# Starting six weight buffers at different offsets modulo 256 bytes

## Chip, cores and metric

The kernel runs on one core of a Trainium2 chip. The metric is the device time of one execution in microseconds (us), the median of several runs. PE is TensorE's matmul side, PEld its weight loads, DVE VectorE, ACT ScalarE, POOL GpSimd, SP the engine that issues most DMAs.

## What is computed

Two transformer blocks on one sequence of 256 positions and 2048 channels, all in 32-bit floats. The first has a hybrid mixer (pooling and a gated delta net), cross attention to a memory of 256 positions and a gated feed-forward; the second has adaptive norms from a conditioning vector, a mixer of two sparse attentions, and a feed-forward with a squared relu. Cut to its products with the large weights:

```python
p = h @ w_in                                   # 2048 x 5136, first mixer
x = x + concat([y_pool, y_dn]) @ w_mix_out
x = x + attention(h @ w_xq, mem_h @ w_xkv) @ w_xo
x = x + (silu(dwconv(h @ w_gate)) * (h @ w_up)) @ w_down     # width 5632
p2 = h2 @ w_in_2 ; x = x + gate * norm(mixers(p2) @ w_o_2)
x = x + gate * norm(relu(h2 @ w_up_2) ** 2 @ w_down_2)       # width 8192
```

## The kernel before

**Tiling.** A weight matrix is cut into groups of 512 columns and each group into units of two blocks of 128 rows, so a unit is 128 partitions by 1024 floats (512 KB). 880 units come through the same ten buffers: four buffers `w32` as the DMA lands them, three `wh` and three `wl`.

**Split.** Each float is used in two parts, a high part and the rest, so that products in the fast format `F32R` keep the precision. `split_to` (L208) does it for each unit: ACT copies the unit into `wh` rounded to `F32R` (L220), DVE (in six units POOL) writes what is left into `wl` (L222). The activations are split likewise into `A0` to `A3` (`act_pair(0)`) or `A4` to `A7` (`act_pair(1)`, and the hidden layers of both feed-forwards); two of each four hold the high parts, two the low ones.

**Products.** `take` (L229) hands a unit to one of two loops. Each product is three matmuls: high by high, high by low, low by high.

```python
mm(ps, wb, h, ...)       # lin_b, L320: weights stationary (128 columns), activations moving (256 columns)
mm(ps, wb, lo, ...)      # L321
mm(ps, wb2, h, ...)      # L322: wb2 is of wl
mm(ps, h, wh[:, k, :], ...)   # lin_a, L302: activations stationary (128 columns), weights moving (512 columns)
mm(ps, h, wl[:, k, :], ...)   # L303
mm(ps, lo, wh[:, k, :], ...)  # L304
```

Every matmul has a weight load of its own, which reads its stationary operand from SBUF beside the moving operand of the matmul before it. A unit holds 24 matmuls of `lin_b` or 12 of `lin_a`. `lin_b` makes the inputs of the mixers, the queries, the memory's keys and the feed-forwards' first layers; `lin_a` makes the rest, above all the feed-forwards' second layers.

**Order.** The order is written out by hand: `take` splits two units ahead (`SPLIT_AHEAD`) and issues loads seven ahead (`LOAD_AHEAD`), and after each unit `pump` lets side tasks (evacuations, attention, norms) issue a few instructions.

**Addresses.** Pools hand out SBUF in the order in which tags are first used. The pool `s` holds activations and small tiles; behind it stand `wh`, `wl` and `w32`. `pad` (L119) takes space that nothing uses, at three places, and `col` (L123) takes a column tile of a few floats. Activations, weight blocks and rows inside these buffers are whole multiples of 256 bytes long, so all that is read of a buffer begins at the buffer's own offset modulo 256.

Of the kernel before, what the change touches and what calls it, by code (L numbers as in the profile page):

```python
# [9 lines left out]
F32 = mybir.dt.float32  # L10
F32R = mybir.dt.float32r
# [4 lines left out]
P = 128  # L16
T = 256
D = 2048
KB = D // P
# [71 lines left out]
class Prog:  # L91
# [24 lines left out]
        self.seq += 1  # L116
        return self.pool.tile(shape, dt, tag=tag, name=f"{tag}_{self.seq}")

    def pad(self, name, n):  # L119

        return self.pool.tile([P, n], F32, tag=name, name=name)

    def col(self, name, n):  # L123
        return self.pool.tile([P, n], F32, tag=f"c_{name}", name=f"c_{name}")

# [85 lines left out]
    def split_to(self, n):  # L211
        nc = self.nc
        while self.split < min(n, len(self.units)):
            u = self.split
            g, kb, nk = self.units[u]
            m = nk * g.n
            src = self.w32.pop(u)
            hi = self.wpool.tile([P, 1024], F32R, tag="wh", name=f"wh_{u}")
            lo = self.wpool.tile([P, 1024], F32R, tag="wl", name=f"wl_{u}")
            nc.scalar.activation(hi[:, :m], src[:, :m], AF.Copy)  # L220
            eng = nc.gpsimd if u in self.relief else nc.vector
            eng.tensor_tensor(lo[:, :m], src[:, :m], hi[:, :m].bitcast(F32), op=OP.subtract)  # L222
            self.whl[u] = (hi[:, :m].rearrange("p (k c) -> p k c", k=nk),
                           lo[:, :m].rearrange("p (k c) -> p k c", k=nk))
            self.split += 1
# [275 lines left out]
    def run(self):  # L501
# [65 lines left out]
        self.mhalf = self.pool.tile([P, 8], F32, name="mhalf")  # L567
        nc.gpsimd.memset(self.mhalf, -0.5)
        nc.scalar.activation(self.col("first", 8), self.mhalf, AF.Copy)
        self.pad("pad0", 48)  # L570


        self.split_to(1)
# [37 lines left out]
        st = self.start(stats())  # L611
        A4 = self.t("A4", [P, 2, 4, T])
        A5 = self.t("A5", [P, 2, 4, T])
        self.pad("pad1", 32)
        S = [{"k": A4[:, 0], "q": A4[:, 1], "v": A5[:, 0]}, {}]
        self.z = [None, None]
        self.dnc = None
# [1216 lines left out]
    def ffn2(self):  # L1834
        nc = self.nc
        xh, xl, ready = self.h2
        ada = self.start(self.ada((5,), ["r4", "r5", "r6", "r7"], ["r8", "r11"], 1024), rate=0.25)
        F = [None] * 4
        fp = self.parts("f_p")
        self.pad("pad2", 48)  # L1840
        hid = {}

        def ups(s):
            hid[s] = self.hidden(["A4", "A6"] if s % 2 else ["A5", "A7"])
            for c in range(2 * s, 2 * s + 2):
                self.lin_b(self.up2[c], xh, xl, lambda a, c=c: self.relu_evac(a, c, hid[s]),
                           ready=ready if c == 0 else None)

        def first(a, c):
            F[c] = self.t(f"r{c}", [P, 2, 512])  # L1850
            yield from self.copy2_evac(a, F[c])

        gr = None
        ups(0)
        for s in range(8):
            if s < 7:
                ups(s + 1)
            if s == 6:
                self.need(ada)
                gp = self.col("GP", KB)  # L1860
                nc.vector.tensor_tensor(gp, self.mod[:, 5], self.par("post_norm_ffn_2"), op=OP.mult)
                gr = self.start(self.gain_rows(gp, ["r9", "r10"]))
            h, l = hid.pop(s)
            for c in range(4):
                if s == 0:
                    evac = lambda a, c=c: first(a, c)
                elif s < 7:
                    evac = lambda a, c=c: self.add2_evac(a, F[c])
                else:
                    evac = lambda a, c=c: self.gain_evac(a, F[c], c, fp, gr)  # L1870
                ev = self.lin_a(self.down2[s][c], lambda kb: h[:, kb], lambda kb: l[:, kb], evac)
        self.need(ev)
        rf = self.rms_cols("f_r", fp)
        dst = self.o["out"][0].rearrange("(b p) d -> p b d", p=P)
        for c in range(4):
            for tb in range(2):
                x = self.X[:, tb, c * 512:(c + 1) * 512]
                if tb and c % 2:
                    nc.gpsimd.tensor_scalar(F[c][:, tb], F[c][:, tb], rf[:, tb:tb + 1], 1.0, op0=OP.mult, op1=OP.mult)
                    nc.gpsimd.tensor_tensor(x, F[c][:, tb], x, op=OP.add)  # L1880
                else:
                    nc.vector.scalar_tensor_tensor(x, F[c][:, tb], rf[:, tb:tb + 1], x, op0=OP.mult, op1=OP.add)
                (nc.sync, nc.scalar)[tb].dma_start(dst[:, tb, c * 512:(c + 1) * 512], x)
# [55 lines left out]
```

## Time and profile before

| what | us |
|---|---|
| median of 3 runs (lowest, highest) | 2738.88 (2733.89, 2740.66) |
| the profiled execution | 2742.97 |
| its span, first to last instruction | 2741.2 |
| PE busy | 2683.0 |
| PEld busy | 2475.7 |
| DVE busy | 1848.6 |
| ACT busy | 1300.0 |
| POOL busy | 289.9 |

Outside the span lie 1.8 us. Matmuls overlap in the pipeline: a matmul of 256 columns is recorded with some 280 ns while the next one starts some 115 ns later. So the pace is read from starts, not from durations. The granted TensorE clock averaged 0.993 of 2.4 GHz.

### The profile page before, as it was taken

The page shows a single profiled execution, that of the slowest core. Times are in us where ns is not written, and L with a number is a line of the kernel's source. Part 1 is how long each engine was busy: PE and PEld are TensorE (multiplying, and loading weights), DVE is VectorE, ACT ScalarE, POOL GpSimd, SP SyncE. Part 2 cuts the span into 40 slices and gives each one's busy share as a digit, 9 for nine tenths or more (in the row PEclk, how much of TensorE's full clock was granted, in tenths as well). Part 3 has the DMA queues.
Part 4 walks back from the last instruction along what each step waited for, and adds up shares of the span by engine and source line. Part 5 has one row for each costly group of instructions (what it writes and reads, how often), then busy time and mean ns, then how long its engine had stood idle before and what let it go on. Part 6 is the DMA issues. An engine that isn't in the chain of part 4 may idle for free.

```text
span 2741.2 us, 45609 instructions
## 1 busy us (share of the span) xinstructions
PE 2683.0 (98%) x18322; PEld 2475.7 (90%) x18322; DVE 1848.6 (67%) x2276; ACT 1300.0 (47%) x1894; POOL 289.9 (11%) x249
## 2 busy tenths in 40 slices
PE   8999999999999999999999989999989999999997
PEld 8999998889989999999999789998879988999896
DVE  6665745677787877777877576677576566655556
ACT  6544533454455455444444454444554444444443
POOL 0230201000001020000000031101121000000020
PEclk9999999999999999999999999999999999999999
DMA  8644544688787877877877745443557767665554
GB/s 289 200 127 133 187 124 139 221 293 273 230 269 263 273 259 256 282 261 271 277 264 257 216 148 178 152 141 125 178 174 239 238 217 241 232 190 190 192 185 145
DMA packets 292116, 584.29 MB, mean 213 GB/s; under 512 B 23968, under 2 KB 32288, under 8 KB 291904
## 3 DMA queue, kind: packets, MB, share of 16 engines
q1 hardware_dynamic: 287952, 569.93, 63.5%
q0 software_dynamic: 3232, 10.14, 1.2%
q8 instruction: 143, 2.34, 0.3%
q10 hardware_dynamic: 720, 1.31, 0.1%
q14 instruction: 69, 0.57, 0.1%
HBM read 579.21 MB, written 2.10 MB: 212 GB/s over the span
## 4 chain that ended last, share of the span: by engine, by line
PE 89%; issue 6%; DVE 2%; ACT 1%; POOL 1%; DMA 0%; SPq 0%; DVEq 0%; ACTq 0%; POOLq 0%
PE acc L320 16%; PE acc L321 16%; PE acc L322 16%; PE acc L302 11%; PE acc L303 11%; PE acc L304 11%; PE m L992 1%; DVE wl L222 1%; PE m L1045 1%; PE m L1052 1%; ACT wh L220 1%; PE m L1142 1%; PE m L1111 1%; PE m L995 0%; DMA w<-w_in 0%
## 5 line engine op out<-in xcount | busy, mean ns | idle before, releaser
L222 DVE TENSOR_TENSOR wl<-w,wh 128x1024 fp32r<-128x1024 f32 x874 | 1094.3, 1254 | 826.4 <-ACT wh L220 820.0
L220 ACT ACTIVATE wh<-w 128x1024 fp32r<-128x1024 f32 x880 | 928.6, 1059 | 1152.7 <-PE acc L321 618.6
L320 PE MATMUL acc<-A,wh 128*128 128x256 f32 x3968 | 1125.1, 284 | 11.4 <-ACT A L406 7.7
L322 PE MATMUL acc<-A,wl 128*128 128x256 f32 x3968 | 1113.4, 281 | 6.1 <-POOL wl L222 3.3
L321 PE MATMUL acc<-A,wh 128*128 128x256 f32 x3968 | 1113.6, 281 | 0.4 <-DVE A L407 0.2
L320 PEld LDWEIGHTS acc<-A,wh 128*128 128x128 f32 x3968 | 752.0, 190 | 13.4 <-ACT A L406 7.7
L322 PEld LDWEIGHTS acc<-A,wl 128*128 128x128 f32 x3968 | 757.4, 191 | 6.7 <-POOL wl L222 3.7
L321 PEld LDWEIGHTS acc<-A,wh 128*128 128x128 f32 x3968 | 750.5, 189 | 2.2 <-DVE A L1406 0.6
L302 PE MATMUL acc<-wh,A 128*128 128x512 f32 x1536 | 608.6, 396 | 3.5 <-ACT wh L220 3.2
L303 PE MATMUL acc<-wl,A 128*128 128x512 f32 x1536 | 600.9, 391 | 2.2 <-DVE wl L222 2.2
L304 PE MATMUL acc<-wh,A 128*128 128x512 f32 x1536 | 600.6, 391 | 0.0
L303 PEld LDWEIGHTS acc<-wl,A 128*128 128x128 f32 x1536 | 289.4, 188 | 63.0 <-DVE wl L222 5.2
L302 PEld LDWEIGHTS acc<-wh,A 128*128 128x128 f32 x1536 | 289.1, 188 | 62.6 <-ACT wh L220 3.6
L304 PEld LDWEIGHTS acc<-wh,A 128*128 128x128 f32 x1536 | 289.1, 188 | 61.1
L1194 DVE SCALAR_TENSOR_TENSOR r<-r,c_silu_c,r 128x1024 f32<-128x1024 f32 x128 | 170.0, 1328 | 0.0
L1828 POOL TENSOR_TENSOR s<-s 128x512 f32<-128x512 f32 x32 | 51.0, 1593 | 557.2 <-ACT s L1827 557.2
L1194 DVE SCALAR_TENSOR_TENSOR s<-s,c_silu_c,s 128x512 f32<-128x512 f32 x128 | 95.8, 749 | 13.4 <-DMA s<-w_ada 11.6
L1249 POOL TENSOR_TENSOR r<-r,rr 128x1024 f32<-128x1024 f32 x11 | 27.9, 2534 | 571.8 <-ACT r L1248 529.0
L1672 ACT ACTIVATE s<-s,c_am 128x128 f32<-128x128 f32 (+1 forms) x48 | 21.5, 448 | 92.2 <-DVE c_am L1670 92.2
L1560 POOL TENSOR_TENSOR r<-r,s 128x512 f32<-128x512 f32 x15 | 25.5, 1703 | 227.4 <-DVE s L1557 227.4
L1245 DVE SCALAR_TENSOR_TENSOR r<-r,prm,r 128x254 f32<-128x254 f32 x88 | 42.3, 481 | 1.6
L378 ACT ACTIVATE dd<-X 128x512 bf16<-128x512 f32 x40 | 25.1, 627 | 23.2 <-DVE X L441 15.8
(368 smaller groups left out, 1634.7 us busy)
## 6 DMA issues: line engine op xcount, KB each, us to landing
w<-w_up SPq DMA_DIRECT2D x216, 512.0 KB, 3.7
w<-w_down SPq DMA_DIRECT2D x216, 512.0 KB, 4.0
w<-w_in SPq DMA_DIRECT2D x152, 512.0 KB, 3.5
r<-w_ada SPq DMA_DIRECT2D x128, 512.0 KB, 5.0
w<-w_gate SPq DMA_DIRECT2D x88, 512.0 KB, 4.3
w<-w_xkv SPq DMA_DIRECT2D x64, 512.0 KB, 3.9
s<-w_ada SPq DMA_DIRECT2D x128, 256.0 KB, 5.0
w<-w_mix_out SPq DMA_DIRECT2D x32, 512.0 KB, 3.6
```

The source lines that it names most:

```text
L220: nc.scalar.activation(hi[:, :m], src[:, :m], AF.Copy)
L222: eng.tensor_tensor(lo[:, :m], src[:, :m], hi[:, :m].bitcast(F32), op=OP.subtract)
L302: mm(ps, h, wh[:, k, :], start=kb == 0, stop=False)
L303: mm(ps, h, wl[:, k, :], start=False, stop=False)
L304: mm(ps, lo, wh[:, k, :], start=False, stop=kb == g.nkb - 1)
L320: mm(ps, wb, h, start=kb == 0 and b % 2 == 0, stop=False, skip_group_check=True)
L321: mm(ps, wb, lo, start=False, stop=False, skip_group_check=True)
L322: mm(ps, wb2, h, start=False, stop=kb == g.nkb - 1, skip_group_check=True)
L1194: nc.vector.scalar_tensor_tensor(acc, tiles.pop(n), self.silu_c[:, kb:kb + 1], acc, op0=OP.mult, op1=OP.add)
L1245: nc.vector.scalar_tensor_tensor(cv[:, b, s:], st[:, b, :T - s], w[k], cv[:, b, s:], op0=OP.mult, op1=OP.add)
L1249: nc.gpsimd.tensor_tensor(cv, cv, self.rr[:, None, :].to_broadcast([P, 4, T]), op=OP.mult)
L1828: nc.gpsimd.tensor_tensor(y, y, y, op=OP.mult)
```

## The change

The `wh` and `wl` buffers become 1040 floats long instead of 1024; only the first 1024 are used. The three pads go. To keep `A0` to `A7` where they were, five column tiles that the kernel needs later (`G1`, `G2`, `GP`, `silu_c`, `gl16`) are taken early, in the place of the first two pads.

```diff
-    def pad(self, name, n):
-
-        return self.pool.tile([P, n], F32, tag=name, name=name)
...
-            hi = self.wpool.tile([P, 1024], F32R, tag="wh", name=f"wh_{u}")
-            lo = self.wpool.tile([P, 1024], F32R, tag="wl", name=f"wl_{u}")
+            hi = self.wpool.tile([P, 1040], F32R, tag="wh", name=f"wh_{u}")
+            lo = self.wpool.tile([P, 1040], F32R, tag="wl", name=f"wl_{u}")
...
-        self.pad("pad0", 48)
+        for name in ("G1", "G2", "GP"):
+            self.col(name, KB)
...
-        self.pad("pad1", 32)
+        for name in ("silu_c", "gl16"):
+            self.col(name, KB)
...
-        self.pad("pad2", 48)
```

Every engine runs the same instructions in the same order with the same waits. What differs is where buffers begin. In bytes modulo 256, by the addresses in the two built programs:

| buffer | before | after |
|---|---|---|
| `A0` to `A3` | 128 | 128 |
| `A4` to `A7` | 192 | 192 |
| `wh` of units 0, 1, 2 (then in turn) | 192, 192, 192 | 192, 64, 0 |
| `wl` of units 0, 1, 2 (then in turn) | 192, 192, 192 | 128, 0, 192 |
| `w32` (all four) | 192 | 64 |

The large tiles of the pool `s` keep their addresses; of the small column tiles some move.

## Rows read from the trace of the kernel before

**Rows 1.** The page's span and busy times: engine, us, share, instructions.

```profile
span 2741.2 us, 45609 instructions
PE 2683.0 (98%) x18322; PEld 2475.7 (90%) x18322; DVE 1848.6 (67%) x2276; ACT 1300.0 (47%) x1894; POOL 289.9 (11%) x249
```

**Rows 2.** The page's chain that ended last, by engine.

```profile
PE 89%; issue 6%; DVE 2%; ACT 1%; POOL 1%; DMA 0%; SPq 0%; DVEq 0%; ACTq 0%; POOLq 0%
```

**Rows 3.** The page's costliest groups: xcount, busy us, mean ns, idle before by releaser.

```profile
L222 DVE TENSOR_TENSOR wl<-w,wh 128x1024 fp32r<-128x1024 f32 x874 | 1094.3, 1254 | 826.4 <-ACT wh L220 820.0
L220 ACT ACTIVATE wh<-w 128x1024 fp32r<-128x1024 f32 x880 | 928.6, 1059 | 1152.7 <-PE acc L321 618.6
L320 PE MATMUL acc<-A,wh 128*128 128x256 f32 x3968 | 1125.1, 284 | 11.4 <-ACT A L406 7.7
...
L302 PE MATMUL acc<-wh,A 128*128 128x512 f32 x1536 | 608.6, 396 | 3.5 <-ACT wh L220 3.2
```

**Rows 4.** PE's waits: us in total, times, longest us.

```profile
PE acc L302 <- ACT wh L220: 3.2, 1, 3.2
PE acc L322 <- DVE wl L222: 2.8, 1, 2.8
...
PE acc L303 <- DVE wl L222: 2.2, 4, 0.8
```

**Rows 5.** Timeline of PE, lin_b on A0 to A3: start us, us, what.

```profile
2049.80 0.28 PE L320 MATMUL acc<-A,wh 128*128 128x256 f32 x1
2049.91 0.28 PE L321 MATMUL acc<-A,wh 128*128 128x256 f32 x1
...
2069.97 0.28 PE L321 MATMUL acc<-A,wh 128*128 128x256 f32 x1
```

**Rows 6.** The same, in another stretch of lin_b on A0 to A3.

```profile
1009.79 0.28 PE L320 MATMUL acc<-A,wh 128*128 128x256 f32 x1
1009.90 0.28 PE L321 MATMUL acc<-A,wh 128*128 128x256 f32 x1
...
1029.93 0.28 PE L320 MATMUL acc<-A,wh 128*128 128x256 f32 x1
```

**Rows 7.** Groups by line from 2050 to 2070 us: xcount, busy us, mean ns.

```profile
L321 PE MATMUL acc<-A,wh 128*128 128x256 f32 x60 | 16.6, 276 | 0.0
...
L322 PEld LDWEIGHTS acc<-A,wl 128*128 128x128 f32 x60 | 11.3, 188 | 0.0
```

**Rows 8.** The same from 1010 to 1030 us.

```profile
L321 PE MATMUL acc<-A,wh 128*128 128x256 f32 x57 | 16.0, 281 | 0.0
L322 PEld LDWEIGHTS acc<-A,wl 128*128 128x128 f32 x57 | 11.0, 192 | 0.0
```

**Rows 9.** Stretches of lin_b on A0 to A3: PE busy us, matmuls, PEclk, DMA.

```profile
1140.00:1160.00 20.00, 20.00 (x172) 1.00 0.79 266
1310.00:1330.00 20.00, 20.00 (x178) 1.00 0.79 269
```

**Rows 10.** Timeline of PE, lin_b on A4 to A7 (the memory's keys).

```profile
318.52 0.28 PE L322 MATMUL acc<-A,wl 128*128 128x256 f32 x1
...
326.54 0.28 PE L320 MATMUL acc<-A,wh 128*128 128x256 f32 x1
```

**Rows 11.** Timeline of PE, lin_a on A4 to A7.

```profile
2679.76 0.39 PE L303 MATMUL acc<-wl,A 128*128 128x512 f32 x1
...
2709.90 0.39 PE L304 MATMUL acc<-wh,A 128*128 128x512 f32 x1
```

**Rows 12.** Timeline of PE, lin_a on A0 to A3.

```profile
479.83 0.39 PE L302 MATMUL acc<-wh,A 128*128 128x512 f32 x1
...
509.82 0.39 PE L304 MATMUL acc<-wh,A 128*128 128x512 f32 x1
```

**Rows 13.** Timeline of PE, lin_a on A4 to A7, behind a wait.

```profile
970.41 0.47 PE L302 MATMUL acc<-wh,A 128*128 128x512 f32 x1 [0.31 <-DVE r L1258]
970.72 0.39 PE L303 MATMUL acc<-wl,A 128*128 128x512 f32 x1
...
972.80 0.39 PE L303 MATMUL acc<-wl,A 128*128 128x512 f32 x1
...
973.93 0.39 PE L302 MATMUL acc<-wh,A 128*128 128x512 f32 x1
```

## The prediction

> **What bounds the kernel now.** I read the busy times first: PE works 98% of the span, DVE 67%, ACT 47% [rows 1]. The chain of waits agrees: 89% of what ended last is PE [rows 2]. So time can come only from PE's own pace, or from a wait that PE doesn't have today. The groups by line say where the pace matters: L320 to L322 (`lin_b`) are 3 x 3968 = 11,904 matmuls of 256 columns, L302 to L304 (`lin_a`) are 3 x 1536 = 4,608 of 512 columns [rows 3]. A change of 1 ns per matmul is 11.9 us in the first and 4.6 us in the second.
>
> Then I read the pace in the timeline, from starts. A `lin_b` on A0 to A3 runs at one of two paces: 178 steps in 2069.97 - 2049.80 = 20.17 us, 113.3 ns each [rows 5], or 171 steps in 1029.93 - 1009.79 = 20.14 us, 117.8 ns each [rows 6]. The code is the same and the granted clock is full (2.4 GHz) in both kinds [rows 9]. The slower kind has longer records: matmuls of 281 ns against 276, and the load for L322 takes 192 ns against 188 [rows 7, 8]. So a load and the matmul that streams beside it do hold each other up, for whole stretches at a time. Counting matmuls in ten stretches of 20 us spread over the span, six have 172 or 173 and four have 178 or 179; one of each kind stands in [rows 9]. Their mean pace is (6 x 117.8 + 4 x 113.3) / 10 = 116.0 ns.
>
> **The pace goes with where the two reads begin.** Call D the start of what is loaded less the start of what is moving, modulo 256. Before, `lin_b` on A0 to A3 has D = 192 - 128 = 64, always. The one `lin_b` on A4 to A7, the memory's keys (4 groups x 16 blocks x 4 x 3 = 768 matmuls), has D = 0: 67 steps in 326.54 - 318.52 = 8.02 us, 119.7 ns, slower than either pace of D = 64 [rows 10]. In `lin_a` it is the other way round. On A4 to A7 D is 0: 133 steps in 30.14 us, 226.6 ns [rows 11]. On A0 to A3 D is 128 - 192 = 192: 131 steps in 29.99 us, 228.9 ns [rows 12]. And D = 0 has to settle first: behind a wait, nine steps take 972.80 - 970.72 = 2.08 us, 231.1 ns each, and the next five take 1.13 us, 226 ns [rows 13]. That D is the cause is my inference; the stretches differ in their side work too.
>
> **What the change moves.** No instruction, order or wait changes, so there is no term for added or removed work, and no queue is passed. The buffers' starts change D. For `lin_b` on A0 to A3 (11,904 - 768 = 11,136 matmuls) the three units in turn have D = 64, 0, 64, then 192, 128, 192, then 128, 64, 128 within a block's three matmuls: of nine, three at 64, one at 0, three at 128, two at 192. For the memory's keys it is three at 0, three at 64, two at 128, one at 192. For `lin_a` on A4 to A7 it is three at 0, one at 64, two at 128, three at 192, and it changes from matmul to matmul; on A0 to A3 one at 0, two at 64, three at 128, three at 192. By the code the gate and output of the first mixer and the values of the second run on A0 to A3, 864 of the `lin_a` matmuls, so 3,744 run on A4 to A7.
>
> *lin_b on A0 to A3.* D = 128 and 192 have no row in `lin_b`. Their bounds are 113.3 and 119.7 ns, the ends of all that I see; I take the 116.0 of D = 64, the other offset that isn't 0. One in nine goes to 119.7. That is 116.0 + 3.7 / 9 = 116.4 ns, so 0.41 x 11,136 = +4.6 us. Bounds: all at 113.3 gives -2.7 x 11,136 = -30.1 us, all at 119.7 gives +3.7 x 11,136 = +41.2 us.
>
> *The memory's keys.* (3 x 119.7 + 6 x 116.0) / 9 = 117.2 ns, so -2.5 x 768 = -1.9 us; bounds -6.4 x 768 = -4.9 us and 0.
>
> *lin_a on A4 to A7.* Today it settles at its best pace within some ten matmuls [rows 13] and stays there. After, D changes at each matmul and its pattern every 12, when a unit ends, so the settled pace hardly has time to form. Ends: 226.6 ns as now, and 231.1 as in the run-in. I take 228.9, the pace at D = 192 and about their middle: +2.3 x 3,744 = +8.6 us; bounds 0 and +4.5 x 3,744 = +16.8 us.
>
> *lin_a on A0 to A3.* It has no settled best pace to lose; I leave it at 228.9. Bounds: 226.6 and 231.1, so -2.0 and +1.9 us.
>
> *The split, the loads and the small tiles.* L220 and L222 read and write at other offsets. Their price is hidden: DVE waits 820 us in all for L220 and ACT 619 us for L321 [rows 3], while PE waits for the two only 3.2 + 2.8 + 2.2 us [rows 4]. To be felt, a split would have to grow by the idle time before it, about 826.4 / 874 = 0.9 us on DVE, on an instruction of 1.25 us [rows 3]. Without that cover a slower L222 would cost its growth 880 times. I take nothing for these.
>
> The sum is +4.6 - 1.9 + 8.6 + 0 = +11.3 us. It is made on the profiled execution: 2742.97 + 11.3 = 2754.3 us. That execution lies 4.1 us above the median of the three runs, so against the median it is 2738.88 + 11.3 = **2750 us**, 0.4% slower. The bounds of all terms add to -37.0 us (2702) and +59.9 us (2799).
>
> **A rule that speaks against all this.** By the Trainium skill (TensorE: Matmul & The Clock Gate, Part 2, step 1, on LDWEIGHTS) TensorE reads SBUF through two independent ports, so "Loading the next tile's weights doesn't steal SBUF read bandwidth from the running matmul"; by that, starts couldn't matter, and the sum would be 0 us. The trace doesn't agree: the two paces, with loads of 188 and 192 ns, are of the same code at the same clock [rows 7, 8].
>
> **The rivals.**
> - *No change, 2739 us.* The paces come from what happens behind each wait, not from D, and each kind of matmul keeps its mix. For it: the two paces occur at one and the same D [rows 5, 6]. Against it: D = 0 is at neither of the two [rows 10]. The rule above has this result.
> - *Faster, 2722 us.* The 117.8 ns pace of `lin_b` lives on the same D at every matmul, for tens of microseconds; where D changes within each block and at each unit, it can't hold. Then D other than 0 costs 113.3: `lin_b` on A0 to A3 goes to (8 x 113.3 + 119.7) / 9 = 114.0 ns, -2.0 x 11,136 = -22.3 us; the keys to 115.4, -3.3 us; `lin_a` still loses 8.6: -17.0 us. It decides where `lin_b` falls under 116.0 - (8.6 - 1.9) / 11,136 = 115.4 ns. For it: the 113.3 ns pace is there in four stretches of ten. Against it: that pace also needs to hold, and it gets no longer than the other.
> - *Much slower, 2774 us.* The offsets that I haven't seen keep `lin_b` at 117.8 ns throughout: +1.8 x 11,136 = +20.0 us, and `lin_a` stays in its run-in: +16.8 us; with the keys -1.9, that is +34.9 us. For it: the run-in is slow for ten matmuls of a unit's 12. Against it: nothing shows 128 to be bad.
>
> **How the numbers follow.** The forecast has 0.34, with a range of its own from 2742 to 2765 (the `lin_a` term from end to end, `lin_b` by half a nanosecond); no change 0.22, faster 0.28, much slower 0.16. The range has to reach to both sides: 2712 to 2780 leaves out the outer third of the faster case and some 0.1 of the upper ones. A measurement of this kernel can tell 0.3%, 8.2 us, from no change. About 0.06 of the forecast's chance and 0.03 of the faster case lie within that, so faster is 0.25, same 0.31, slower 0.44.
>
> **What would show it.** In the changed kernel's timeline, starts of `lin_a` on A4 to A7 should stand 228 to 230 ns apart instead of 226.6, with a pattern that repeats every 36 matmuls, three units; if they stay at 226.6, that step is wrong. In `lin_b` long stretches at 113.3 and 117.8 should have given way to one mix near 116.4; long stretches at either pace would say that D isn't what chooses the pace, and a mean under 115.4 is the faster case. Loads of `lin_b` should show 188 and 192 ns mixed within each unit. L220 and L222 should keep about 1.06 and 1.25 us; if they grow by more than 0.9 us, PE's waits for them will grow, and the prediction is wrong on a term that I set to nothing.

## The result and the profile after

The changed kernel takes **2766.43 us** (median of 4 runs, 2765.67 to 2767.38), the kernel before beside it 2738.32 us. The ratio is 1.0105, with a 95% interval from 1.0087 to 1.0122: 28 us slower. The forecast of 2750 us had the sign right and the size two and a half times too small.

The page of the changed kernel: its span and busy times, its chain by engine, and its costliest groups. They answer to [rows 1 to 3]; the numbers of code lines are smaller by 4.

```profile
span 2764.4 us, 45609 instructions
PE 2709.1 (98%) x18322; PEld 2486.5 (90%) x18322; DVE 1849.1 (67%) x2276; ACT 1300.4 (47%) x1894; POOL 291.3 (11%) x249
...
PE 88%; issue 6%; DVE 3%; ACT 2%; POOL 1%; DMA 1%; SPq 0%; DVEq 0%; ACTq 0%; POOLq 0%
...
L218 DVE TENSOR_TENSOR wl<-w,wh 128x1024 fp32r<-128x1024 f32 x874 | 1092.1, 1251 | 849.9 <-ACT wh L216 848.3
L216 ACT ACTIVATE wh<-w 128x1024 fp32r<-128x1024 f32 x880 | 928.6, 1058 | 1176.4 <-PE acc L317 628.0
L316 PE MATMUL acc<-A,wh 128*128 128x256 f32 x3968 | 1128.2, 284 | 11.3 <-ACT A L402 7.8
...
L298 PE MATMUL acc<-wh,A 128*128 128x512 f32 x1536 | 614.9, 400 | 3.3 <-ACT wh L216 3.1
```

The same 45,609 instructions run. DVE, ACT and POOL are busy within 1.4 us of what they were, and the split costs the same: 1251 ns for the rest (1254 before), 1058 ns for the high part (1059 before). DVE has 23.5 us more idle time ahead of L218 (849.9 - 826.4), about what the span grew by (23.2 us): the split waits for a slower PE. TensorE alone is busier: PE by 26.1 us and its loads (PEld) by 10.8. PE's waits for the split, the answer to [rows 4] (us in all, times, longest):

```profile
PE acc L298 <- ACT wh L216: 3.1, 1, 3.1
PE acc L318 <- DVE wl L218: 2.7, 1, 2.7
...
PE acc L299 <- DVE wl L218: 1.6, 3, 0.8
```

They are as small as before. So the time lies in PE's own pace. Three of ten stretches of `lin_b` on A0 to A3, the answer to [rows 9] (PE busy us, matmuls, clock, DMA share, GB/s):

```profile
864.00:884.00 20.00, 20.00 (x173) 1.00 0.78 261
1320.00:1340.00 20.00, 20.00 (x173) 1.00 0.77 260
2628.00:2648.00 20.00, 20.00 (x173) 1.00 0.60 185
```

Before, six of the ten had 172 or 173 matmuls and four had 178 or 179. Now all ten have 173, at a DMA load from 185 to 261 GB/s and full granted clock. PE's timeline (start us, record us, what), the first and last of 173 matmuls of `lin_b`, then of 131 of `lin_a` on A4 to A7; they answer to [rows 5, 6, 11]:

```profile
1029.73 0.28 PE L317 MATMUL acc<-A,wh 128*128 128x256 f32 x1
...
1049.90 0.28 PE L318 MATMUL acc<-A,wl 128*128 128x256 f32 x1
```

```profile
2699.83 0.39 PE L299 MATMUL acc<-wl,A 128*128 128x512 f32 x1
...
2729.96 0.40 PE L300 MATMUL acc<-wh,A 128*128 128x512 f32 x1
```

`lin_b`: 20.17 us in 172 steps, 117.3 ns. `lin_a`: 30.13 us in 130 steps, 231.8 ns, where it was 226.6. Over the whole trace (the mean of all steps from one start to the next, those over 140 or 260 ns left out because they hold a wait):

| matmuls | before, ns | after, ns | steps | difference, us |
|---|---|---|---|---|
| `lin_b` on A0 to A3 | 116.2 | 117.4 | 11,136 | +13.6 |
| `lin_a` on A4 to A7 | 227.1 | 231.6 | 3,744 | +16.5 |
| `lin_a` on A0 to A3 | 229.4 | 231.6 | 864 | +1.9 |
| memory's keys | 119.8 | 117.8 | 768 | -1.5 |

The differences are made from unrounded means. They add to 30.5 us, where the span grew by 23.2 us in this pair of executions: the steps left out add to 331.5 us before and 323.5 us after. The median grew by 28.1 us.

### The profile page after: what moved, and what is told of

Its sections match the earlier page's. It is cut to its first block, busy times and chain, and to the rows that moved or that the text cites. A ratio compares the mean times of both kernels' runs of the same rounds, so it can differ in the third digit from the quotient of the medians.

```text
span 2764.4 us, 45609 instructions
## 1 busy us (share of the span) xinstructions
PE 2709.1 (98%) x18322; PEld 2486.5 (90%) x18322; DVE 1849.1 (67%) x2276; ACT 1300.4 (47%) x1894; POOL 291.3 (11%) x249
## 4 chain that ended last, share of the span: by engine, by line
PE 88%; issue 6%; DVE 3%; ACT 2%; POOL 1%; DMA 1%; SPq 0%; DVEq 0%; ACTq 0%; POOLq 0%
PE acc L316 16%; PE acc L317 15%; PE acc L318 15%; PE acc L298 11%; PE acc L299 11%; PE acc L300 11%; DVE wl L218 1%; PE m L990 1%; PE m L1043 1%; ACT wh L216 1%; PE m L1050 1%; PE m L1109 0%; PE m L1140 0%; PE m L993 0%; PE m L1698 0%
## 5 line engine op out<-in xcount | busy, mean ns | idle before, releaser
L218 DVE TENSOR_TENSOR wl<-w,wh 128x1024 fp32r<-128x1024 f32 x874 | 1092.1, 1251 | 849.9 <-ACT wh L216 848.3
L216 ACT ACTIVATE wh<-w 128x1024 fp32r<-128x1024 f32 x880 | 928.6, 1058 | 1176.4 <-PE acc L317 628.0
L316 PE MATMUL acc<-A,wh 128*128 128x256 f32 x3968 | 1128.2, 284 | 11.3 <-ACT A L402 7.8
L318 PE MATMUL acc<-A,wl 128*128 128x256 f32 x3968 | 1113.0, 280 | 6.3 <-POOL wl L218 3.6
L316 PEld LDWEIGHTS acc<-A,wh 128*128 128x128 f32 x3968 | 750.0, 189 | 13.1 <-ACT A L402 7.8
L318 PEld LDWEIGHTS acc<-A,wl 128*128 128x128 f32 x3968 | 749.0, 189 | 6.9 <-POOL wl L218 4.0
```

Source lines behind the costliest of these rows:

```text
L316: mm(ps, wb, h, start=kb == 0 and b % 2 == 0, stop=False, skip_group_check=True)
L318: mm(ps, wb2, h, start=False, stop=kb == g.nkb - 1, skip_group_check=True)
```

## Experiments

D is, as in the prediction, the start of what is loaded less the start of what is moving, modulo 256. In each run below the arithmetic and the order are those of the two kernels; only addresses differ. The expectations name theories by numbers or letters. Theory 1 is that each D has a pace of its own, whatever the matmul before; V takes that theory's paces, as the first four runs measured them, and counts how often each D comes up. M adds a price for a D that changes from matmul to matmul. P, S and H are forms of one other idea, that a change of D at some place can bring the stream to its better pace.

### One D at a time: u0, u64, u128

The kernel before, with `pad2` left out, or cut to 16 or 32 floats: all weight buffers start at 0, 64 or 128 instead of 192. The edit of u64:

```diff
-        self.pad("pad2", 48)
+        self.pad("pad2", 16)
```

> The kernel before with its third pad taken out: all ten weight buffers begin at 0 instead of 192, the same for all. lin_b on A0 to A3 then always has D = 128, lin_a on A4 to A7 always D = 192. Theory 1 (each D has its own pace, mixed or not): lin_b at the 117.6 ns that D = 128 shows in the changed kernel, +1.4 ns x 11,136 = +16 us; lin_a at the 228.9 ns of D = 192 in the kernel before, +2.3 x 3,744 = +9 us; sum about 2763 us. Theory 2 (only a D that changes from matmul to matmul costs, any constant D settles): within 8 us of before, 2730 to 2746 us, with lin_a at 226.6 ns.

> The kernel before with its third pad 128 bytes shorter: all ten weight buffers begin at 64. lin_b on A0 to A3 always has D = 192, lin_a on A4 to A7 always D = 128. Theory 1 (each D has its own pace): lin_b at the 116.2 ns that D = 192 shows in the changed kernel, 0 us; lin_a at the 231.9 ns of D = 128 there, +4.8 x 3,744 = +18 us; about 2756 us. Theory 2 (only a changing D costs): 2730 to 2746 us.

> The kernel before with its third pad 64 bytes shorter: all ten weight buffers begin at 128. lin_b on A0 to A3 always has D = 0, lin_a on A4 to A7 always D = 64. Theory 1 (each D has its own pace): lin_b at the 119.7 ns of the memory's keys in the kernel before, +3.5 x 11,136 = +39 us; lin_a at 229.6 ns, the pace of D = 64 in the changed kernel, +2.5 x 3,744 = +9 us; about 2786 us. Theory 2 (only a changing D costs): 2730 to 2746 us.

Measured: u0 2775.08 us, ratio 1.0128 [1.0112, 1.0144]; u64 2774.76, 1.0125 [1.0108, 1.0142]; u128 2795.83, 1.0205 [1.0189, 1.0222]. PE's timelines in one stretch of each loop. u0, 169 matmuls of `lin_b`, then 89 of `lin_a`:

```profile
1029.77 0.28 PE L322 MATMUL acc<-A,wl 128*128 128x256 f32 x1
...
1049.92 0.28 PE L322 MATMUL acc<-A,wl 128*128 128x256 f32 x1
...
2709.78 0.39 PE L303 MATMUL acc<-wl,A 128*128 128x512 f32 x1
...
2729.92 0.39 PE L304 MATMUL acc<-wh,A 128*128 128x512 f32 x1
```

u64, 173 of `lin_b`, then 88 of `lin_a`:

```profile
1029.73 0.28 PE L322 MATMUL acc<-A,wl 128*128 128x256 f32 x1
...
1049.99 0.28 PE L320 MATMUL acc<-A,wh 128*128 128x256 f32 x1
...
2709.68 0.40 PE L302 MATMUL acc<-wh,A 128*128 128x512 f32 x1
...
2729.90 0.39 PE L302 MATMUL acc<-wh,A 128*128 128x512 f32 x1
```

u128, 169 of `lin_b`, then 88 of `lin_a`:

```profile
1029.78 0.28 PE L322 MATMUL acc<-A,wl 128*128 128x256 f32 x1
...
1049.94 0.28 PE L322 MATMUL acc<-A,wl 128*128 128x256 f32 x1
...
2724.64 0.39 PE L302 MATMUL acc<-wh,A 128*128 128x512 f32 x1
...
2744.93 0.40 PE L302 MATMUL acc<-wh,A 128*128 128x512 f32 x1
```

These stretches give 119.9, 117.8 and 120.0 ns for `lin_b` (20.15 / 168, 20.26 / 172, 20.16 / 168) and 228.9, 232.4 and 233.2 ns for `lin_a` (20.14 / 88, 20.22 / 87, 20.29 / 87). With the means over the whole traces there is a table that no row of before could give:

| D | `lin_b` on A0 to A3, ns | memory's keys (`lin_b` on A4 to A7), ns | `lin_a` on A4 to A7, ns | `lin_a` on A0 to A3, ns |
|---|---|---|---|---|
| 0 | 119.9 (u128) | 119.8 (before) | 227.1 (before) | 228.1 (u128) |
| 64 | 116.2 (before: 113.3 and 117.8 mixed) | 116.7 (u0) | 233.3 (u128) | 233.3 (u64) |
| 128 | 119.1 (u0) | 118.7 (u64) | 232.8 (u64) | 232.6 (u0) |
| 192 | 117.5 (u64) | 117.8 (u128) | 229.1 (u0) | 229.4 (before) |

The two columns of each loop reach the same D from different starts, so a row's two values come from different runs; they lie within 0.5 ns in `lin_b` and 1.0 ns in `lin_a`. That speaks for the difference and not for a start by itself.

The kernel before stands on the best value in both main columns. Theory 2 (2730 to 2746 us) falls. Theory 1 holds in kind, but its times of 2763, 2756 and 2786 us were all too low: the paces that it took for single D's out of the mixed trace of the changed kernel were too good, and the unseen offsets cost more than the forecast had given them.

### The rest of the change alone: w32_64

The changed kernel with `wh` and `wl` back at 1024 floats, starting at 192, and a gap of 128 bytes that leaves `w32` at 64. The columns stay where the change put them.

```diff
-            hi = self.wpool.tile([P, 1040], F32R, tag="wh", name=f"wh_{u}")
-            lo = self.wpool.tile([P, 1040], F32R, tag="wl", name=f"wl_{u}")
+            hi = self.wpool.tile([P, 1024], F32R, tag="wh", name=f"wh_{u}")
+            lo = self.wpool.tile([P, 1024], F32R, tag="wl", name=f"wl_{u}")
...
+        self.gap.tile([P, 32], F32, tag="gap", name="gap")
```

> The changed kernel with wh and wl back at 1024 floats, so all six begin at 192 as before; the five column tiles stay early, and 128 unused bytes ahead of w32 make it begin at 64 as in the changed kernel. If the loss comes from the matmuls' reads: 2738 us, within 0.3%. If it comes from where DMA writes and ACT and DVE read w32, or from the moved column tiles: most of the +28 us, so 2755 to 2767 us.

Measured: 2737.93 us, ratio 0.9991 [0.9982, 1.0001]; `lin_b` 115.7 ns, `lin_a` 227.1 ns. DMA landings at 64 instead of 192, the split's reads there and the moved columns cost nothing. The whole 28 us are in the starts of `wh` and `wl`.

### Difference or start: shift64

The kernel before without `pad0`. Everything in the pools moves by 192 bytes: A0 to A3 start at 192, A4 to A7 and all weights at 0, so each D stays as it was.

```diff
-        self.pad("pad0", 48)
```

> The kernel before without its first pad: everything behind it moves by 192 bytes, so A0 to A3 begin at 192, A4 to A7 at 0 and all ten weight buffers at 0. Every start is another, every difference D is as before (64 in lin_b on A0 to A3, 0 in lin_a on A4 to A7). Theory D (the difference of the two starts sets the pace): the paces of before, 116 and 227 ns, and 2730 to 2747 us. Theory A (the start of the weights itself sets it, and 0 is a bad one): the 2775 us of the run with the weights alone at 0.

Measured: 2736.17 us, ratio 0.9991 [0.9982, 1.0001]. u0 has its weights at 0 too, and takes 2775. So that start by itself decides nothing, and the difference does, as in the table above. PE's timeline of shift64: `lin_b` in two stretches (172 and 179 matmuls), and `lin_a` (90):

```profile
1009.75 0.28 PE L321 MATMUL acc<-A,wh 128*128 128x256 f32 x1
...
1029.89 0.28 PE L321 MATMUL acc<-A,wh 128*128 128x256 f32 x1
...
2039.78 0.28 PE L322 MATMUL acc<-A,wl 128*128 128x256 f32 x1
...
2059.95 0.28 PE L320 MATMUL acc<-A,wh 128*128 128x256 f32 x1
...
2669.74 0.39 PE L304 MATMUL acc<-wh,A 128*128 128x512 f32 x1
...
2689.91 0.39 PE L303 MATMUL acc<-wl,A 128*128 128x512 f32 x1
```

117.8 and 113.3 ns (20.14 / 171, 20.17 / 178) are the two paces of [rows 5, 6] again, and 226.6 ns (20.17 / 89) that of [rows 11].

### Half of the change each: lo_only and hi_only

lo_only gives the longer buffers to `wl` alone, hi_only to `wh` alone (with `wl` in a pool of its own, all at 192).

```diff
-            hi = self.wpool.tile([P, 1040], F32R, tag="wh", name=f"wh_{u}")
+            hi = self.wpool.tile([P, 1024], F32R, tag="wh", name=f"wh_{u}")
```

```diff
-            lo = self.wpool.tile([P, 1040], F32R, tag="wl", name=f"wl_{u}")
+            lo = self.wlpool.tile([P, 1024], F32R, tag="wl", name=f"wl_{u}")
```

> One part of the change alone: only the three wl buffers are 64 bytes longer and begin at 192, 64, 0 for units 0, 1, 2; all wh stay at 192. Theory V (each D has the pace that the runs with uniform starts gave it: lin_b 116.0, 117.5, 119.1, 119.9 ns at D = 64, 192, 128, 0; lin_a 227.1, 229.1, 232.8, 233.3 at D = 0, 192, 128, 64; a mix costs the mean of its members): lin_b 116.5 ns, +6 us; lin_a (2 x 227.1 + 229.7) / 3 = 228.0 ns, +3 us; about 2747 us. Theory M (a D that changes within a block costs by itself in lin_a): lin_a at 231.6 ns in two units of three, +11 us, and +6 us for lin_b; about 2756 us.

> The other part alone: only the three wh buffers begin at 192, 64, 0; all wl stay at 192. Theory V: lin_b 117.0 ns (two of three matmuls go with wh), +11 us; lin_a (227.1 + 230.9 + 228.4) / 3 = 228.8 ns, +6 us; about 2756 us. Theory M: lin_a near 231.6 ns in two units of three, so +11 us instead of +6; about 2761 us.

Measured: lo_only 2751.73 us, 1.0051 [1.0034, 1.0068]; hi_only 2756.74, 1.0071 [1.0056, 1.0086]. Against the 2739.12 of before in that series they cost 12.6 and 17.6 us, together 30.2: each half carries its share of the 28. hi_only comes out at V's 2756 us, lo_only between V's 2747 and M's 2756. In lo_only two of three matmuls of a `lin_a` block keep D = 0, and yet `lin_a` goes to 230.2 ns, where the table gives (7 x 227.1 + 232.8 + 229.1) / 9 = 228.0. PE's timeline of lo_only, 87 steps of `lin_a` in 20.01 us, 230.0 ns:

```profile
2694.95 0.39 PE L298 MATMUL acc<-wh,A 128*128 128x512 f32 x1
...
2714.96 0.40 PE L298 MATMUL acc<-wh,A 128*128 128x512 f32 x1
```

In hi_only, where `wh` moves, `lin_a` is at 229.3 ns, 0.5 above the table's 228.8. So in `lin_a` D = 0 loses its pace beside other offsets, by more in lo_only than in hi_only.

### The same D within a unit: by_unit

`wl` in a pool of its own, so that `wh` and `wl` of one unit start alike, at 192, 64 and 0 in turn. `lin_b` then has D = 64, 192, 128 and `lin_a` D = 0, 128, 192, each for a whole unit.

```diff
-            lo = self.wpool.tile([P, 1040], F32R, tag="wl", name=f"wl_{u}")
+            lo = self.wlpool.tile([P, 1040], F32R, tag="wl", name=f"wl_{u}")
...
+        self.gap1.tile([P, 16], F32, tag="gap1", name="gap1")
```

> wh and wl of a unit begin at the same offset, 192, 64, 0 for units 0, 1, 2, so D changes from unit to unit but not within one. Theory V: lin_b (116.0 + 117.5 + 119.1) / 3 = 117.5 ns, +17 us; lin_a (227.1 + 232.8 + 229.1) / 3 = 229.7 ns, +10 us; with the keys -1, about 2764 us. Theory M (changes within a block are what cost beyond the mean): the same 2764 us here, and a lin_a pace in each unit near its uniform one. If changes from unit to unit cost too: lin_a near the 231.6 ns of the changed kernel, about 2771 us.

Measured: 2745.60 us, ratio 1.0031 [1.0018, 1.0044], a clear miss. `lin_a` is at 230.9 ns, above the (227.1 + 232.8 + 229.1) / 3 = 229.7 of the table; its units with D = 0 average 230.3, close to the 231.1 of the run-in, while those with D = 128 and 192 stay near the table, at 232.6 and 229.8. But `lin_b` is at 115.7, below the (116.2 + 117.5 + 119.1) / 3 = 117.6 of the table. PE's timeline of by_unit, four rows 24 matmuls apart, at the changes from one unit's D to the next:

```profile
1022.59 0.28 PE L320 MATMUL acc<-A,wl 128*128 128x256 f32 x1
...
1025.31 0.28 PE L320 MATMUL acc<-A,wl 128*128 128x256 f32 x1
...
1028.14 0.28 PE L320 MATMUL acc<-A,wl 128*128 128x256 f32 x1
...
1030.88 0.28 PE L320 MATMUL acc<-A,wl 128*128 128x256 f32 x1
```

D = 192 takes 2.72 us, 113.3 ns a step; D = 128 takes 2.83 us, 117.9; D = 64 takes 2.74 us, 114.2. In its own run D = 192 had 117.5. Behind a unit with D = 128 the stream comes to 113.3 ns within some four matmuls and keeps it through the two units that follow. Over the whole trace, in units that follow the one before without a wait or another PE instruction, D = 64 is at the better pace, once settled, in all 109, D = 192 in 103 of 106, and D = 128 in none of 108. So Theory 1 is too simple: a pace depends on D and on what the stream comes from.

### Can that be used? act_0_64, lo_at_0, half_at_0, first_128

Four kernels keep the weights at 192 and move the activations instead, by columns or pads between A0 and A3, so that D changes in `lin_b` while `lin_a` on A4 to A7 keeps its 0.

act_0_64 starts A0 and A1 at 0, A2 and A3 at 64 (D = 192, 128, 192 in a block's three matmuls); lo_at_0 starts A2 and A3 at 0 (D = 64, 192, 64).

```diff
+            if j == 2 and not self.placed:
+                self.placed = True
+                self.col("G2", KB)
```

```diff
+            n = {(0, 2): 32}.get((half, j))
...
+                self.pad(f"pad_a{j}", n)
```

> All weight buffers uniform at 192 (1024 floats) as before, but A0, A1 (high activations) begin at 0 and A2, A3 (low ones) at 64 instead of 128. lin_b on them then always has D = 192, 128, 192, which in the changed kernel is one unit of three and runs there at 116.1 ns on average and at 116, 112, 118 when settled. Theory P (the pair of D's within a block sets the pace): lin_b 115.4 to 116.1 ns, -6 to +1 us; lin_a on A0 to A3 gets worse D's, 233 ns x 864 = +3 us; about 2733 to 2742 us. Theory V (mean of the D's alone): (2 x 117.5 + 119.1) / 3 = 118.0 ns, +22 us and +3 us; about 2763 us.

> As before, but the low activations A2, A3 begin at 0 instead of 128. lin_b on A0 to A3 then has D = 64, 192, 64 in each block, the pair that ran at 114.1 ns in one unit of three when only wl was moved; lin_a on A4 to A7 keeps D = 0. Theory P (the pair of D's in a block has its own pace): 113.3 to 114.1 ns, -21 to -30 us, lin_a on A0 to A3 +1 us; 2710 to 2719 us. Theory V (mean of the D's alone): (2 x 116.0 + 117.5) / 3 = 116.5 ns, about 2745 us. Theory S (a pace is kept from matmul to matmul, and only the breaks between units let lin_b out of the slower one): near the 117 ns of a stream that isn't broken, 2740 to 2752 us.

Measured: act_0_64 2756.05 us, 1.0068 [1.0053, 1.0083]; lo_at_0 2757.22, 1.0075 [1.0058, 1.0092]. `lin_b` of lo_at_0, 172 matmuls in the timeline:

```profile
1019.79 0.28 PE L320 MATMUL acc<-A,wh 128*128 128x256 f32 x1
...
1039.93 0.28 PE L320 MATMUL acc<-A,wh 128*128 128x256 f32 x1
```

20.14 us in 171 steps, 117.8 ns, and the mean of both whole traces is 117.8. P falls twice: a change of D within the block brings nothing, and lo_at_0 even loses all of D = 64's better stretches.

half_at_0 starts A1 and A3 at 0, so that D is 64 or 192 for four units at a time.

```diff
+            n = {(0, 1): 32, (0, 2): 32, (0, 3): 32}.get((half, j))
```

> As before, but A1 and A3 (second half of the 16 row blocks) begin at 0: lin_b on A0 to A3 changes between D = 64 and D = 192 every four units, lin_a on A4 to A7 keeps D = 0. Theory S (a change of D between units starts the stream anew, and from there it mostly finds the faster pace, as the units of D = 64 and 192 did at 114.2 and 114.5 ns when the offset went with the unit): 114.4 ns, -18 us, lin_a on A0 to A3 +2 us; about 2722 us. Theory V (mean of the paces at uniform starts): (116.0 + 117.5) / 2 = 116.75 ns, +8 us; about 2748 us.

Measured: 2751.81 us, 1.0054 [1.0039, 1.0069]. D = 64 averages 116.35 ns and D = 192 117.75, as in the table. A change between these two D is no help either, and S falls.

first_128 lets the first two blocks of A0 and A2 start at 64, so that each group begins with one unit of D = 128 and goes on with D = 64.

```diff
+                c = k * T + (16 if half == 0 and kb // 8 == 0 and k > 1 else 0)
```

> All weight buffers at 192 as before, but the first two of the 16 activation blocks in A0 and A2 begin at 64 instead of 128, so the first unit of each lin_b group on A0 to A3 has D = 128 and the other seven D = 64; lin_a on A4 to A7 keeps D = 0. Theory H (which pace a stream takes at D = 64 depends on what it comes from; when the offset went with the unit, the units of D = 64 came from D = 128 and were at 113.3 ns after four matmuls, through the next unit too): (118.4 + 7 x 113.6) / 8 = 114.2 ns, -20 us; about 2718 us, more if side work breaks the stream in between. Theory V (mean of the paces at uniform starts): (119.1 + 7 x 116.0) / 8 = 116.4 ns, +4 us; about 2743 us.

Measured: 2740.08 us, 1.0013 [1.0003, 1.0022]. Its timeline, with changes to D = 128 at the second row and back to D = 64 at the third (43, 24, 44 and 72 steps from row to row):

```profile
2054.81 0.28 PE L319 MATMUL acc<-A,wl 128*128 128x256 f32 x1
...
2059.87 0.28 PE L317 MATMUL acc<-A,wh 128*128 128x256 f32 x1
...
2062.72 0.28 PE L317 MATMUL acc<-A,wh 128*128 128x256 f32 x1
...
2067.74 0.28 PE L319 MATMUL acc<-A,wl 128*128 128x256 f32 x1
...
2075.89 0.28 PE L319 MATMUL acc<-A,wl 128*128 128x256 f32 x1
```

D = 64 runs at 117.7 ns (5.06 us / 43), D = 128 at 118.8 (2.85 / 24), then the same D = 64 at 114.1 and 113.2 (5.02 / 44, 8.15 / 72). Here the passage turns the pace to the better one. At the next group it turns it back (52, 24 and 48 steps):

```profile
2075.89 0.28 PE L319 MATMUL acc<-A,wl 128*128 128x256 f32 x1
...
2081.79 0.28 PE L317 MATMUL acc<-A,wh 128*128 128x256 f32 x1
...
2084.64 0.28 PE L317 MATMUL acc<-A,wh 128*128 128x256 f32 x1
...
2090.29 0.28 PE L317 MATMUL acc<-A,wh 128*128 128x256 f32 x1
```

D = 64 is at 113.5 ns (5.90 / 52), D = 128 at 118.8 (2.85 / 24), and D = 64 behind it at 117.7 (5.65 / 48). It is the same in the whole trace. Of the 58 groups, 29 begin with no wait and no other PE instruction around their first unit, and at all 29 the pace turns, 8 times to the better and 21 times to the worse one. In the kernel before, all of the same 29 keep the pace that they come with. The passage swaps the two paces and doesn't choose the better.

D = 64 averages 115.5 ns here. In runs with D = 64 throughout it is 116.2 (before, an execution 4 us above the median), 115.7 (w32_64) and 115.8 (shift64). Against the last two the gain is 0.2 to 0.3 x 9,700 = 2 to 3 us, and the D = 128 units, at 119.0 ns, take back some 3.2 x 1,390 = 4 us; the run is 3.4 us slower than the kernel before beside it (2736.73). H has the mechanism in part, that a passage through D = 128 changes the pace, and its direction wrong. No kernel here beats the one before.

## Why the prediction was right in part

**What bounds the kernel** was right. PE is busy 98% of the span in both kernels, and each run's time followed PE's two paces.

**D as the cause** was right, and it was called an inference. shift64 (same D, other starts, same time) and u0, u64 and u128 (other D, 36 to 57 us more) show it. What was drawn from the rule that spoke against it, that starts can't matter, falls with them: by the Trainium skill (TensorE: Matmul & The Clock Gate, Part 2, step 1) a load doesn't steal bandwidth from the running matmul, and here starts alone move the kernel from 2736 to 2796 us. What passes between a load and a matmul to make it so, no run here shows. The length of the loads, in which the prediction saw the sign of it, doesn't go with the pace: in the stretches shown above, loads take 188 to 190 ns at 119.9 ns a step (u0), 187 to 188 at 117.8 (u64) and 192 at 120.0 (u128).

**The term for `lin_b` was mis-sized**: +4.6 us forecast, +13.6 measured. The step that failed is the choice of 116.0 ns for D = 128 and 192, "the other offset that isn't 0". Their runs give 119.1 and 117.5. With these, the prediction's own nine matmuls average (3 x 116.2 + 119.9 + 3 x 119.1 + 2 x 117.5) / 9 = 117.9 ns; 117.4 was measured. The visit count was right, the prices were not. (Within a block the order is 64, 64, 0 and so on, and not 64, 0, 64; the counts are the same.) The bound of 119.7 ns that stood beside the choice held for both. The +13.6 us is measured against the traced execution of before; against the 115.7 and 115.8 ns of w32_64 and shift64 it would be some +18 us, and with the 8 us by which the left-out steps became shorter, the sum is then 27 us, near the median's 28.

**The term for `lin_a` on A4 to A7 was mis-sized too**: +8.6 us forecast, +16.5 measured, with 231.6 ns just over the upper bound of 231.1. Two things were added up there. D = 64 and 128 had no row in `lin_a` and cost 233.3 and 232.8, more than the run-in; by the table the nine average (3 x 227.1 + 233.3 + 2 x 232.8 + 3 x 229.1) / 9 = 229.7. And D = 0 does lose its settled pace when its neighbours differ, as the prediction argued: lo_only, by_unit and hi_only lie 2.2, 1.2 and 0.5 ns above the table, the changed kernel 1.9. The prediction saw the second and not the first, and took the middle of a range whose top was too low.

**The small terms** were right or small: the keys -1.5 us (forecast -1.9), the split, loads and columns nothing (w32_64). `lin_a` on A0 to A3, taken at 0, came at its upper bound of +1.9.

**The signs** came as described in kind: one mix in `lin_b` with 173 matmuls in all ten stretches, where there had been two paces. The mean, 117.4, is above the 116.4 looked for, and `lin_a` at 231.6 is above 228 to 230. Its three units in turn average 229.9, 231.5 and 233.3 ns, the pattern of 36 matmuls. The loads of `lin_b` do mix, at 188, 190 and 188 ns on average for L316 to L318 from 1030 to 1050 us.

**The rivals.** "No change" falls by the u runs, though its picture of a pace that is set behind waits fits the two paces of the one D = 64 (see below). "Faster" needed `lin_b` under 115.4 ns and falls at 117.4; its idea that a changing D can free the stream from 117.8 ns was not empty, though, as by_unit shows. "Much slower", at a chance of 0.16, had the paces nearly right (117.8 and 231.1 ns, 2774 us). Its weak point was said to be that nothing shows 128 to be bad; u0 and u64 do show it.

**What stays open** is why D = 64 and 192 have two paces in `lin_b`. When they change is partly seen. Before, w32_64 and shift64 have together 138 runs of 25 or more `lin_b` matmuls on A0 to A3 without a wait or another PE instruction; only one of them shows both paces. So at a constant D the pace changes almost only where something breaks the stream, and a passage through D = 128 turns it without such a break (by_unit, first_128). What decides which pace follows a break was not found. A kernel that changes D only ahead of the slow stretches was not tried.

## What to carry to other kernels

Where PE is the bound and each matmul has a load of its own, the starts of the loaded and the moving buffer modulo 256 are a setting of the kernel: measure the four differences with one pad, for each loop, and then hold the best one constant (steps finer than 64 bytes were not tried). Here the best are 64 for 256 moving columns and 0 for 512, and spreading buffers over all offsets gave the stream the bad ones too. When a prediction needs the price of an offset that no row shows, the price of the nearest one seen, in a kernel that already stands on its best offsets, is the cheap end and no middle.

## What the hardware showed that I had not expected

- The speed of a stream of loads and matmuls depends on the difference of the two starts: 116.2 to 119.9 ns with 256 moving columns, 227.1 to 233.3 with 512, and the best difference is another in each.
- The floors are 113.3 and 226.6 ns, 272 and 544 cycles at 2.4 GHz: 17 cycles for 16 columns in both. No stretch of 24 steps or more, in any trace, ran below them by more than the rounding of the rows.
- One and the same D has two paces, 113.3 and 117.8 ns, each kept for tens of microseconds, and 24 matmuls at another D (128) swapped it at 29 of 29 places, 21 times for the worse.
- Where DMA lands and where ACT and DVE read made no difference at the one other start tried: 2737.9 us with `w32` at 64, 2738.7 beside it with `w32` at 192. Nor did where they write: the split takes 1058 and 1251 ns into the moved buffers of the changed kernel, 1059 and 1254 before.
